# Two-layer GLA and differential-attention network with hierarchical experts: gather banks, order of the opening, and the residual's place

## Chip, cores and metric

One core of a Trainium2 chip runs the whole program. The metric is the device time of one execution in microseconds. TensorE (PE) does the matmuls, VectorE (DVE) and ScalarE (ACT) the elementwise work and the copies out of the matmul accumulators (PSUM), SyncE (SP) issues the DMAs that load the weights, and GpSimd (POOL) does little.

## What is computed

The input is 256 tokens of width 1024, in fp32. Layer 0 mixes tokens by gated linear attention, layer 1 by differential attention on keys and values made from layer 0's output. Behind each mixer stands a layer norm of the scaled residual, then a mixture of 16 experts (two per token, from one of four groups of four), and another residual and norm:

```
for layer in range(DEPTH):                       # DEPTH = 2
    mix = gla_mixer(h, ...) if layer < 1 else diff_attention(h, ..., k1, k2, v, ...)
    h = layer_norm(ALPHA * h + mix, ln_g[layer, 0], ln_b[layer, 0])       # ALPHA = sqrt 2
    ffn = hier_moe(h, ...)
    h = layer_norm(ALPHA * h + ffn, ln_g[layer, 1], ln_b[layer, 1])

def hier_moe(t):                                 # 256 x 1024
    combine = ...                                # 256 x 16, two weights per token
    y = 0
    for e in range(16):
        hdn = silu(t @ w_gate[e]) * (t @ w_up[e])        # 1024 x 512 each
        y = y + combine[:, e:e + 1] * (hdn @ w_down[e])  # 512 x 1024
```

## The kernel before

The mixers take the first 131 us and the stretch from about 365 to 504 us; the change does not touch them. The rest is the function moe, once per layer.

**One expert.** Each expert has a block of 64 slots. A one-hot matrix OH says which token sits in which slot. Of an expert, PE does, in this order: the transposes of the expert before's scatter matrix and hidden values (s_prep L594 and tr_part L626, into PSUM banks of tag pC), the first quarter of its gate and up products (gu_part L610, j = 0, into a bank of tag pB), the down product of the expert before (down_part L638, one pB and one pC bank), the other three quarters of gate and up, and the scatter of the expert before (L670: four matmuls that add the product o into the four accumulators y of tag pA, which stay open through all experts). DVE and ACT make silu and the product (L617, L619), copy transposes out (L629), and split the down product into a rounded high and a low part o (ACT L646, DVE L647), since fp32r matmuls keep only the high part. PE runs its instructions in program order. The loop at L766 issues all this; "with after(x)" puts an instruction behind x in the order. An fp32 matmul leaves two records in the profile, an fp32r one (gather, scatter, broadcasts) one. Expert matmuls use half of the array's columns, c = 0 and c = 1, and two of them, one on each half, run side by side.

**The gather.** For every four experts gather_group (L538) makes their inputs xg: 32 matmuls of the split x (tile xs: high part by ACT L534, low part by DVE L535, four buffers) with OH, in eight steps k of four (high and low part of each token half), two steps to a bank. Of each bank DVE copies one half out (L562), then ACT the other (L560). It stands at the opening of moe and behind the transposes in the iterations e = 4, 8 and 12; in layer 1 the last gather also makes the inputs of a seventeenth block (five blocks, one step to a bank). All these banks are of tag pC, of which there are two; pB has two as well, used in turn by gate and up products and down products. At the opening, DVE makes the first token half of OH (L519), the low parts of the first four xs, then the second half of OH.

**The residual.** ALPHA times the normed input must be added to y. At e = 5 the generator residual (L408) rebuilds it in the tile xr: eight broadcast matmuls of the norm's weights (bcast_row L203, two per bank, four banks of pC), each bank read by two DVE instructions (L417 or L419), then the subtraction of the mean (L424). Then, for each of its four blocks of 512 columns, ACT L809 writes a high part and DVE L810 a low part into two tiles of tag o (two buffers, shared with the down products), and two identity matmuls L812 add them to y.

**Weights.** SP loads an expert as six tiles of 1 MB (four for gate and up in two DMAs each, two for down), into a ring of 16 slots; three spare tiles x0 to x2 take weights 16 to 18 of each layer and are free afterwards. A slot's next load starts when PE has read its last one. So weights come in as PE uses them up.

## Time and profile before

| | us |
|---|---|
| median of 3 runs | 770.43 (769.76 to 772.49) |
| the profiled execution | 771.24 |
| its span, first to last instruction | 769.3 |
| PE busy | 727.1 (95%) |
| DVE busy | 357.4 (46%) |
| ACT busy | 296.8 (39%) |
| experts of layer 0, opening gather to last scatter | 132 to 366 |
| experts of layer 1 | 504 to 758 |

PE is busy nearly everywhere, so idle time alone says little: a busy PE includes pairs that run one by one. The better measure is the distance from one expert's scatter to the next, which is the same for all ordinary experts, and what stands between where it is longer. In the rows further down, x16 counts records, a time in brackets is the idle time before a group and what ended it, PEclk is the clock granted to TensorE as a share of full speed, and the DMA share is the mean busy share of the core's 16 DMA engines.

### The profile page before, as it was taken

To read this page: it belongs to the slowest core of one execution; us is meant where nothing else is said; L and a number is where in the kernel's file an instruction comes from. 1 tells how busy PE (TensorE), PEld (TensorE's weight loads), DVE (VectorE), ACT (ScalarE), POOL (GpSimd) and SP (SyncE) were. 2 spreads that over 40 slices of the span, in tenths; PEclk is the share of its full clock that TensorE was granted. 3 is DMA by queue.
4 is the path that set the end of the run, shared out by engine and by line. 5 is a ranking of instruction groups with operands and counts; after the bars stand their busy time and mean duration, and the time that the engine had idled before them with its cause. 6 is when DMAs were issued, how large, how long until landed. Compare 5 with 4: busy or idle time off the path is not lost. (4 is left out here: it accounts for less than half of the span.)

```text
span 769.3 us, 10560 instructions
## 1 busy us (share of the span) xinstructions
PE 727.1 (95%) x3743; PEld 407.8 (53%) x3743; DVE 357.4 (46%) x959; ACT 296.8 (39%) x651; POOL 8.9 (1%) x21
## 2 busy tenths in 40 slices
PE   7999998999999999999999999999999999999993
PEld 5898776434333434434798877753343343343331
DVE  3655766333263332322758877654235332332225
ACT  4554766323212322222666656552232232232123
POOL 2200000000000000000000000000000000000000
PEclk9999999999999999999999999999999999999997
DMA  7999957599999999999999355619999999999951
GB/s 226 312 384 388 337 191 262 181 397 394 367 387 392 393 396 395 393 393 367 290 364 359 111 174 209 220 62 389 394 381 395 393 363 384 395 395 393 392 200 55
DMA packets 131934, 247.57 MB, mean 322 GB/s; under 512 B 7932, under 2 KB 38117, under 8 KB 131750
## 3 DMA queue, kind: packets, MB, share of 16 engines
q1 hardware_dynamic: 131270, 244.68, 87.6%
q0 software_dynamic: 176, 1.59, 0.5%
q8 instruction: 31, 0.51, 0.3%
q10 hardware_dynamic: 432, 0.59, 0.2%
q14 instruction: 25, 0.20, 0.1%
HBM read 245.77 MB, written 2.63 MB: 323 GB/s over the span
## 5 line engine op out<-in xcount | busy, mean ns | idle before, releaser
L610 PE MATMUL pB<-W,xg 128*64 128x512 f32 x1056 | 263.6, 600 | 0.0
L610 PEld LDWEIGHTS pB<-W,xg 128*64 128x64 f32 x1056 | 77.3, 138 | 137.9 <-issue 132.3
L638 PE MATMUL pB<-W,ht 128*64 128x512 f32 x248 | 112.6, 594 | 0.0
L638 PE MATMUL pC<-W,ht 128*64 128x512 f32 x248 | 111.5, 592 | 0.0
L647 DVE SCALAR_TENSOR_TENSOR o<-pB,wst,o 64x512 fp32r<-64x512 f32 x31 | 23.1, 744 | 145.3 <-ACT o L646 145.3
L119 DVE TENSOR_TENSOR lo<-W,hi 128x512 fp32r<-128x512 f32 x96 | 66.4, 696 | 37.0 <-PE pA L128 23.9
L118 ACT ACTIVATE hi<-W 128x512 fp32r<-128x512 f32 x96 | 59.3, 629 | 48.3 <-PE pA L129 27.8
L646 ACT ACTIVATE o<-pB,wst 64x512 fp32r<-64x512 f32 x31 | 21.2, 682 | 129.6 <-PE pC L638 101.8
L619 DVE TENSOR_TENSOR hd<-sl,pB 128x256 f32<-128x256 f32 x33 | 13.9, 421 | 102.5 <-ACT sl L617 102.5
L617 ACT ACTIVATE sl<-pB 128x256 f32<-128x256 f32 x33 | 12.7, 385 | 126.0 <-PE pB L610 126.0
L638 PEld LDWEIGHTS pB<-W,ht 128*64 128x64 f32 x248 | 33.3, 137 | 52.4 <-issue 49.3
L553 PE MATMUL pC<-OH,xs 128*128 128x256 f32 (+1 forms) x256 | 39.7, 308 | 7.4 <-DVE ht L629 3.8
L670 PE MATMUL pA<-o,st 128*128 128x512 f32 x132 | 40.9, 431 | 4.3 <-DVE o L664 2.1
L553 PEld LDWEIGHTS pC<-OH,xs 128*128 128x128 f32 x256 | 34.8, 203 | 17.8 <-DVE ht L629 5.2
L638 PEld LDWEIGHTS pC<-W,ht 128*64 128x64 f32 x248 | 33.9, 137 | 19.4 <-issue 18.2
L670 PEld LDWEIGHTS pA<-o,st 128*128 128x128 f32 x132 | 22.4, 191 | 33.3 <-issue 23.5
L129 PE MATMUL pA<-x1Thi,lo 128*128 128x256 f32 x128 | 36.1, 288 | 1.4 <-DVE lo L119 1.2
L127 PE MATMUL pA<-x1Thi,hi 128*128 128x256 f32 x128 | 36.7, 288 | 0.0
L128 PE MATMUL pA<-x1Tlo,hi 128*128 128x256 f32 x128 | 36.2, 284 | 0.0
L128 PE MATMUL pA<-lo,xThi 128*128 128x384 f32 (+1 forms) x96 | 34.3, 357 | 0.0
L129 PE MATMUL pA<-hi,xTlo 128*128 128x384 f32 (+1 forms) x96 | 34.3, 357 | 0.0
L127 PE MATMUL pA<-hi,xThi 128*128 128x384 f32 (+1 forms) x96 | 34.2, 362 | 0.0
(338 smaller groups left out, 1086.2 us busy)
## 6 DMA issues: line engine op xcount, KB each, us to landing
W<-in_moe_w_gate_dram SPq DMA_DIRECT2D x132, 512.0 KB, 11.2
W<-in_moe_w_up_dram SPq DMA_DIRECT2D x132, 512.0 KB, 11.0
W<-in_moe_w_down_dram SPq DMA_DIRECT2D x66, 1024.0 KB, 12.0
W<-in_a_w_in_dram SPq DMA_DIRECT2D x16, 256.0 KB, 5.6
W<-in_a_w_in_dram SPq DMA_DIRECT2D x4, 1024.0 KB, 17.8
W<-in_a_w_out_dram SPq DMA_DIRECT2D x4, 1024.0 KB, 14.4
W<-in_kv_w_dram SPq DMA_DIRECT2D x4, 1024.0 KB, 8.8
W<-in_b_w_q_dram SPq DMA_DIRECT2D x16, 256.0 KB, 5.4
```

What stands on the lines that cost most here:

```text
L118: act.activation(hi, src, AF.Copy)
L119: dve.tensor_sub(lo, src, hi)
L127: pe.matmul(o, l[0], r[0], start=first, stop=False, skip_group_check=skip)
L128: pe.matmul(o, l[0], r[1], start=False, stop=False, skip_group_check=skip)
L129: pe.matmul(o, l[1], r[0], start=False, stop=last, skip_group_check=skip)
L553: pe.matmul(o, xs[k][:, q // 2, q % 2], OH[g][:, q % 2].rearrange("p e s -> p (e s)"), start=q == 0, stop=q == 3)
L610: mm = pe.matmul(p[c * m:c * m + m, 0:2 * fw].rearrange("p (g f) -> p g f", g=2), xg(k), w[:, :, kk, c * fw:c * fw + fw], start=k == 0, st ...
L619: anchor[1] = dve.tensor_mul(h, sl, p[:, fw:2 * fw])
L638: mm = pe.matmul(p[2 * c // nt][c * m:c * m + m, 0:w], ht[:, q % n, (q // n) * m:(q // n) * m + m], wd_[q // 2][:, q % 2, c * w:c * w + w] ...
L646: act.activation(hi, src, AF.Copy, scale=ws[a:a + m, 0:1])
L647: dve.scalar_tensor_tensor(lo, src, ws[a:a + m, 0:1], hi, op0=ALU.mult, op1=ALU.subtract)
L670: mm = pe.matmul(y[b][c], st[:, b * 128:b * 128 + 128], o[c], start=False, stop=last, skip_group_check=True)
```

## The change

Four edits, all in moe and residual:

1. gather_group takes its banks in the order pB, pB, pC, pC (and again from the start for the gather of five).
2. At the opening, the low parts of xs 1 to 3 are issued behind the second half of OH.
3. The matmuls of down_part are chained in their order, so that its pB and pC products always alternate.
4. The residual is spread. Its first four steps (columns 0 to 511) stand behind the transposes of e = 5, the rest behind those of e = 6; their broadcasts use pB and pC in turn. The high and low parts of one token block (512 KB of fp32r) go to a spare tile rs, block 0 at e = 6 and block 1 at e = 7, and are added by four identity matmuls each (L805) behind the scatters in the iterations e = 7 and e = 8. The tag o is no longer used for it.

```diff
--- before.py
+++ after.py
@@ -405,13 +405,13 @@
         dve.tensor_scalar(gsub, pb[:, P_GS:P_GS + 1], 1.0 - LAM0, None, op0=ALU.mult)
         return nlam, gsub
 
-    def residual(idx, dst):
+    def residual(idx, dst, tiles=(pC, pC)):
 
         s = sm([128, 2, 2], "hsum2")
         for h in range(2):
             hs = slice(h * 512, h * 512 + 512)
             for i in range(2):
-                p = bcast_row(8 * i + 2 * idx + h, pC)
+                p = bcast_row(8 * i + 2 * idx + h, tiles[i])
                 for b in range(2):
                     if i == 0:
                         dve.scalar_tensor_tensor(dst[:, b, hs], xa[:, b, hs], ALPHA, p, op0=ALU.mult, op1=ALU.mult)
@@ -526,13 +526,16 @@
 
             lows = []
 
-            def split_x(k, eng, hold=None):
+            def split_x(k, eng, hold=None, later=False):
 
                 t = mp.tile([128, 2, 2, 128], F32R, tag="xs", bufs=4, name=nm("xs"))
                 x_ = xa[:, :, k * 128:k * 128 + 128]
                 with after(hold):
                     act.activation(t[:, 0], x_, AF.Copy)
-                lows.append(eng.tensor_sub(t[:, 1], x_, t[:, 0]))
+                low = lambda: lows.append(eng.tensor_sub(t[:, 1], x_, t[:, 0]))
+                if later:
+                    return t, low
+                low()
                 return t
 
             def gather_group(g, hold=None, xs=()):
@@ -545,7 +548,9 @@
                 xs = list(xs)
                 for k in range(KC):
                     if n == 5 or k % 2 == 0:
-                        p = pC()
+
+                        i = k if n == 5 else k // 2
+                        p = pC() if i // 2 % 2 else pB()
                     if k >= len(xs):
                         xs.append(split_x(k, dve, hold))
                     o = p[:, 0:320] if n == 5 else p[:, k % 2 * 256:k % 2 * 256 + 256]
@@ -633,10 +638,12 @@
 
                 m, n, w = 128 // nt, 4 // nt, D // nt
                 p = [pB(), pC()]
+                mm = None
                 for q in range(4):
                     for c in range(nt):
-                        mm = pe.matmul(p[2 * c // nt][c * m:c * m + m, 0:w], ht[:, q % n, (q // n) * m:(q // n) * m + m], wd_[q // 2][:, q % 2, c * w:c * w + w],
-                                  start=q == 0, stop=q == 3)
+                        with after(mm):
+                            mm = pe.matmul(p[2 * c // nt][c * m:c * m + m, 0:w], ht[:, q % n, (q // n) * m:(q // n) * m + m], wd_[q // 2][:, q % 2, c * w:c * w + w],
+                                            start=q == 0, stop=q == 3)
                 warm(filler, mm)
                 o = [mp.tile([128, 512], F32R, tag="o", bufs=2, name=nm("o"))[0:2 * m] for _ in range(2)]
                 for c in range(nt):
@@ -756,9 +763,16 @@
                 ht, _ = tr_part(act_part(p, 2), 2)
                 scatter(st, down_part(wdn, ht, wsx, 2)[0], True)
 
-            xs0 = [split_x(k, dve) for k in range(4)]
+            xs0, rest = [split_x(0, dve)], []
+            for k in range(1, 4):
+                t, low = split_x(k, dve, later=True)
+                xs0.append(t)
+                rest.append(low)
             act.activation(sm([128, 2], "warm"), xs0[3][:, 0, 0, 0:2], AF.Exp, scale=0.0)
-            one_hot(0)
+
+            with after(one_hot(0)):
+                for low in rest:
+                    low()
             gather_group(0, None, xs0)
             with after(lows[3]):
                 cw = combine()
@@ -784,6 +798,11 @@
                 with after(mm):
                     if prev is not None:
                         mm = scatter(prev[1], o, False)
+                    if e in (7, 8):
+
+                        with after(mm):
+                            for i in range(4):
+                                mm = pe.matmul(y[e - 7][i // 2], ident_r, rs[:, i // 2, i % 2], start=False, stop=False, skip_group_check=True)
                     with after(mm):
                         sp_ = s_prep(lambda b: OH[g][:, b, e - 4 * g], 64, cw[:, :, e] if e < E else extra[2], anchor)
                     with after(sp_[2]):
@@ -798,18 +817,25 @@
                 if e in (1, 5, 9):
                     held[e + 3] = anchor[0], anchor[1]
                 if e == 5:
+
                     xr = spare_tile(2, [128, 2, D], F32, "xr")
-                    for _ in residual(2 * layer, xr):
-                        pass
-
-                    for b in range(2):
-                        for h in range(2):
-                            v = xr[:, b, h * 512:h * 512 + 512]
-                            hi, lo = (mp.tile([128, 512], F32R, tag="o", bufs=2, name=nm("res")) for _ in range(2))
-                            act.activation(hi, v, AF.Copy)
-                            dve.tensor_sub(lo, v, hi)
-                            for a in (hi, lo):
-                                pe.matmul(y[b][h], ident_r, a, start=False, stop=False, skip_group_check=True)
+                    steps = residual(2 * layer, xr, (pB, pC))
+                    with after(mm):
+                        for _ in range(4):
+                            next(steps)
+                if e == 6:
+                    with after(mm):
+                        for _ in steps:
+                            pass
+                if e in (6, 7):
+                    b = e - 6
+                    rs = spare_tile(1, [128, 2, 2, 512], F32R, "rs")
+                    for h in range(2):
+                        v = xr[:, b, h * 512:h * 512 + 512]
+                        with after(anchor[0] if e == 7 else None):
+                            act.activation(rs[:, h, 0], v, AF.Copy)
+                        with after(anchor[1] if e == 7 else None):
+                            dve.tensor_sub(rs[:, h, 1], v, rs[:, h, 0])
                 if e == 9 and layer:
                     gb = spare_tile(0, [128, 2, 2, 512], F32, "gb")
                     for i in range(2):
```

The order of DVE at the opening of layer 0, before (posm gives the slot of each token, xs_1696 to 1705 are the four split tiles):

```order
L510 SCALAR_TENSOR_TENSOR posm_1694<-sel_1685,pC_1688 128x32
L519 TENSOR_TENSOR OH_1710<-posm_1694,cb 128x256
L535 TENSOR_TENSOR xs_1696<-xa,xs_1696 128x256
L535 TENSOR_TENSOR xs_1699<-xa,xs_1699 128x256
L535 TENSOR_TENSOR xs_1702<-xa,xs_1702 128x256
L535 TENSOR_TENSOR xs_1705<-xa,xs_1705 128x256
L519 TENSOR_TENSOR OH_1710<-posm_1694,cb 128x256
```

and after:

```order
L510 SCALAR_TENSOR_TENSOR posm_1694<-sel_1685,pC_1688 128x32
L519 TENSOR_TENSOR OH_1707<-posm_1694,cb 128x256
L535 TENSOR_TENSOR xs_1696<-xa,xs_1696 128x256
L519 TENSOR_TENSOR OH_1707<-posm_1694,cb 128x256
L535 TENSOR_TENSOR xs_1699<-xa,xs_1699 128x256
L535 TENSOR_TENSOR xs_1701<-xa,xs_1701 128x256
L535 TENSOR_TENSOR xs_1703<-xa,xs_1703 128x256
```

The second OH row has moved from behind four xs rows to behind one.

The order of PE at the second gather (e = 4, layer 0), before:

```order
L594 MATMUL pC_1999<-ident_r,ohw_1996 128x128 x2
L626 MATMUL pC_2006<-ident_r,hd_1990 128x128 x2
L553 MATMUL pC_2015<-OH_2011,xs_2016 128x256 x4
L553 MATMUL pC_2015<-OH_2011,xs_2023 128x256 x4
L553 MATMUL pC_2032<-OH_2011,xs_2033 128x256 x4
L553 MATMUL pC_2032<-OH_2011,xs_2040 128x256 x4
L610 MATMUL pB_2083<-W_992,xg_2014 64x512
L553 MATMUL pC_2049<-OH_2011,xs_2050 128x256 x4
L553 MATMUL pC_2049<-OH_2011,xs_2057 128x256 x4
L553 MATMUL pC_2066<-OH_2011,xs_2067 128x256 x4
L553 MATMUL pC_2066<-OH_2011,xs_2074 128x256 x4
L610 MATMUL pB_2083<-W_992,xg_2014 64x512 x3
```

and after:

```order
L631 MATMUL pC_2006<-ident_r,hd_1990 128x128 x2
L558 MATMUL pB_2015<-OH_2011,xs_2016 128x256 x4
L558 MATMUL pB_2015<-OH_2011,xs_2023 128x256 x4
L558 MATMUL pB_2032<-OH_2011,xs_2033 128x256 x4
L558 MATMUL pB_2032<-OH_2011,xs_2040 128x256 x4
L558 MATMUL pC_2049<-OH_2011,xs_2050 128x256 x4
L558 MATMUL pC_2049<-OH_2011,xs_2057 128x256 x4
L558 MATMUL pC_2066<-OH_2011,xs_2067 128x256 x2
L615 MATMUL pB_2083<-W_992,xg_2014 64x512
L558 MATMUL pC_2066<-OH_2011,xs_2067 128x256 x2
L558 MATMUL pC_2066<-OH_2011,xs_2074 128x256 x4
L615 MATMUL pB_2083<-W_992,xg_2014 64x512 x3
```

The first sixteen gather matmuls now write pB banks, and the lone gate and up matmul of the next expert (W is its weights) stands ten gather matmuls further on.

The order of PE at the residual, in the iteration e = 6 of layer 0, before (o and res share a tag; y is pA_1654 to 1657):

```order
L610 MATMUL pB_2246<-W_1024,xg_2014 64x512 x3
L203 MATMUL pC_2197<-lnr,sel_r 128x256 x2
L203 MATMUL pC_2202<-lnr,sel_r 128x256 x2
L610 MATMUL pB_2246<-W_1024,xg_2014 64x512
L638 MATMUL pB_2251<-W_1020,ht_2193 64x512 x2
L203 MATMUL pC_2207<-lnr,sel_r 128x256 x2
L638 MATMUL pB_2251<-W_1022,ht_2193 64x512
L203 MATMUL pC_2212<-lnr,sel_r 128x256 x2
L638 MATMUL pB_2251<-W_1022,ht_2193 64x512
L638 MATMUL pC_2252<-W_1020,ht_2193 64x512 x2
L638 MATMUL pC_2252<-W_1022,ht_2193 64x512 x2
```

and after:

```order
L203 MATMUL pB_2197<-lnr,sel_r 128x256 x2
L615 MATMUL pB_2207<-W_1024,xg_2014 64x512
L203 MATMUL pC_2202<-lnr,sel_r 128x256 x2
L615 MATMUL pB_2207<-W_1024,xg_2014 64x512 x3
L645 MATMUL pB_2212<-W_1020,ht_2193 64x512
L645 MATMUL pC_2213<-W_1020,ht_2193 64x512
L645 MATMUL pB_2212<-W_1020,ht_2193 64x512
L645 MATMUL pC_2213<-W_1020,ht_2193 64x512
L645 MATMUL pB_2212<-W_1022,ht_2193 64x512
L645 MATMUL pC_2213<-W_1022,ht_2193 64x512
L645 MATMUL pB_2212<-W_1022,ht_2193 64x512
```

Four broadcasts (lnr is the norm's weights) have moved to the next expert; down products alternate between pB and pC. The identity matmuls, which before stood one by one within the gate and up products, now stand behind a scatter, here that of e = 7:

```order
L677 MATMUL pA_1654<-o_2298,st_2254 128x512
L677 MATMUL pA_1655<-o_2299,st_2254 128x512
L677 MATMUL pA_1656<-o_2298,st_2254 128x512
L677 MATMUL pA_1657<-o_2299,st_2254 128x512
L805 MATMUL pA_1654<-rs,ident_r 128x512 x2
L805 MATMUL pA_1655<-rs,ident_r 128x512 x2
L599 MATMUL pC_2331<-ident_r,ohw_2328 128x128 x2
L631 MATMUL pC_2338<-ident_r,hd_2318 128x128 x2
```

The eight matmuls of x2 and x2 rows are split over two experts; the other four stand one expert later. SP's and POOL's orders are unchanged.

## Rows read from the trace of the kernel before

**Rows 1.** The page, busy time, share of the span and instructions of an engine.

```profile
PE 727.1 (95%) x3743; PEld 407.8 (53%) x3743; DVE 357.4 (46%) x959; ACT 296.8 (39%) x651; POOL 8.9 (1%) x21
```

**Rows 2.** Timeline of PE, opening of layer 0 (start us, us, ..., [idle <-releaser]).

```profile
132.64 0.51 PE L553 MATMUL pC<-OH,xs 128*128 128x256 f32 x2
134.27 3.36 PE L553 MATMUL pC<-OH,xs 128*128 128x256 f32 x14 [1.12 <-DVE OH L519]
...
138.65 2.18 PE L553 MATMUL pC<-OH,xs 128*128 128x256 f32 x16
140.75 0.65 PE L610 MATMUL pB<-W,xg 128*64 128x512 f32 x2
```

**Rows 3.** Timeline of DVE, same stretch.

```profile
132.46 1.42 DVE L535 TENSOR_TENSOR xs<-xa,xs 128x256 fp32r<-128x256 f32 x4
133.80 0.41 DVE L519 TENSOR_TENSOR OH<-posm,cb 128x256 fp32r<-128x256 f32 x1
```

**Rows 4.** Windows of 6 us: busy us per engine, PEclk, DMA share, GB/s.

```profile
132.00:138.00 6.00, 4.85 (x20) 3.79 (x19) 4.18 (x15) 3.52 (x8) 0.00 (x0) 0.72 0.01 3
...
330.00:336.00 6.00, 6.00 (x32) 2.50 (x30) 2.21 (x6) 0.95 (x3) 0.00 (x0) 1.00 1.04 396
...
606.00:612.00 6.00, 4.14 (x13) 2.55 (x14) 3.16 (x6) 2.03 (x5) 0.00 (x0) 0.72 1.02 401
```

**Rows 5.** Timeline of PE, layer 0, second gather.

```profile
185.28 1.21 PE L670 MATMUL pA<-o,st 128*128 128x512 f32 x4
...
187.55 2.18 PE L553 MATMUL pC<-OH,xs 128*128 128x256 f32 x16 [0.63 <-DVE ht L629]
189.71 1.07 PE L610 MATMUL pB<-W,xg 128*64 128x512 f32 x2
190.72 2.17 PE L553 MATMUL pC<-OH,xs 128*128 128x256 f32 x16
...
203.26 0.98 PE L670 MATMUL pA<-o,st 128*128 128x512 f32 x3
```

**Rows 6.** Timeline of PE, layer 1, the gather of five blocks.

```profile
684.91 1.64 PE L553 MATMUL pC<-OH,xs 128*128 128x320 f32 x8 [0.45 <-ACT xg L560]
```

**Rows 7.** Timeline of PE, the residual's experts in layer 0, then layer 1.

```profile
215.29 1.21 PE L670 MATMUL pA<-o,st 128*128 128x512 f32 x4
...
218.73 0.72 PE L203 MATMUL pC<-lnr,sel_r 64*128 64x256 f32 x4
...
237.44 1.51 PE L670 MATMUL pA<-o,st 128*128 128x512 f32 x4 [1.06 <-DVE o L647]
...
267.76 1.21 PE L670 MATMUL pA<-o,st 128*128 128x512 f32 x4
...
586.74 1.21 PE L670 MATMUL pA<-o,st 128*128 128x512 f32 x4
...
640.26 1.19 PE L670 MATMUL pA<-o,st 128*128 128x512 f32 x4
```

**Rows 8.** The residual's splits by line: count, ns min/median/max, starts, form.

```profile
L809 ACT ACTIVATE res<-xr x8: 621/629/632, 225.5 to 606.0; 128x512 fp32r<-128x512 f32 x8
...
L810 DVE TENSOR_TENSOR res<-xr,res x8: 684/691/695, 226.4 to 606.6; 128x512 fp32r<-128x512 f32 x8
```

**Rows 9.** SP's queue: issues of late weight loads, layer 0, then layer 1.

```profile
340.42 0.60 SPq L282 DMA_DIRECT2D W<-in_moe_w_up_dram  x1
...
729.15 0.74 SPq L733 DMA_DIRECT2D W<-in_moe_w_down_dram  x1
```

**Rows 10.** DMA issues of these two: KB, us from issue to landing.

```profile
W<-in_moe_w_up_dram SPq DMA_DIRECT2D x1, 512.0 KB, 10.8
...
W<-in_moe_w_down_dram SPq DMA_DIRECT2D x1, 1024.0 KB, 13.0
```

**Rows 11.** Timeline of PE where these two are used.

```profile
352.27 5.32 PE L610 MATMUL pB<-W,xg 128*64 128x512 f32 x24
...
751.67 0.43 PE L658 MATMUL pB<-W,ht 128*64 128x256 f32 x1 [0.63 <-DVE ht L629]
```

## The prediction

> **What bounds the kernel now.** I read the page first: PE is busy 95% of the span [rows 1], so a gain must come out of PE's stream. Then PE's timeline, from one scatter to the next. An ordinary expert takes 12.03 us: 215.29 less 203.26 [rows 5, 7]. An expert with a gather takes 17.98 (185.28 to 203.26) [rows 5], and the three experts from the one with the residual to the third gather of layer 0 take 52.47 (215.29 to 267.76), where three ordinary ones would take 36.09 [rows 7]. In layer 1 the same three take 53.52 (586.74 to 640.26) [rows 7]. These excesses, 5.95, 16.38 and 17.43 us, are what the change can work on, and the opening. Last, the weights: in the middle of the experts the DMA engines have a share of 1.04 and move 396 GB/s [rows 4]. An expert's six tiles are 6.3 MB (six of 1024 KB), so at that rate 15.9 us; PE uses them up in 12.03. So the lead of the weights shrinks from expert to expert, and what is left of it at the end of a layer limits what PE can gain.
>
> **The opening, twice.** PE does two gather matmuls, then waits 1.12 us for the second half of OH, then does fourteen in 3.36 us, and sixteen more in 2.18 [rows 2]. Sixteen in 2.18 are 0.136 each; fourteen should take 1.9. The mean granted clock of these 6 us is 0.72, against 1.00 later [rows 4]: behind the wait PE ran at the lower of its two levels. DVE does four low parts in 1.42 us ahead of that half of OH, which starts at 133.80 [rows 3]. With one ahead of it, it starts at 132.46 + 0.36 = 132.82 and ends by 133.23, so the wait falls to about 0.15. The three low parts behind it end by 134.3; PE needs the last of them about twelve matmuls later. The gather then takes 0.5 (the first two, with the rest of the wait) + 4.4 (32 by 0.136) + 1.0 (the lone gate and up matmul in the middle, 1.01 from 189.71 to 190.72 [rows 5]) = 5.9 from 132.64, to 138.6; before, PE goes on at 140.75 [rows 2]. That is 2.15 us in each layer. Bounds: 1.0 if only OH comes earlier and the clock falls all the same, 2.2 at best.
>
> **The gathers.** The second one waits 0.63 us for the copy of the transposes, because it needs the pC bank that they stand in [rows 5]. Now its first two banks are pB: one held the gate and up product of the expert just finished, which DVE read before the transposes could start, the other a down product of the expert before, long copied. The third bank is pC, but comes 2.17 us later [rows 5]. So 0.6 goes; nothing is late in its place, since the xs and OH are made experts ahead. I take 0.57. The lone matmul stays lone, and stands ten gather matmuls later, so it has more time for the two copies ahead of it. The last gather of layer 0 saves the same. That of layer 1 has eight banks, and besides the 0.63 waits at least once more for ACT, 0.45 [rows 6]: with four banks in turn both should go, 1.0. What it adds: pB now takes turns between gathers and products, and the first product of the expert reuses the first gather bank. That is costed among the rivals.
>
> **The residual and the third gather.** Before: 16.38 us of excess in layer 0, of which 5.95 is the gather. The rest is four broadcast matmuls of 0.18 (0.72 for four [rows 7]) and two more pairs inside the down product, whose halves then run alone instead of in pairs; eight identity matmuls one by one among the gate and up products; and at the end the scatter waits 1.06 for the down product's low part [rows 7], since the splits of the residual stand ahead of it and share its two tiles. Layer 1 loses 1.05 more, and there the clock is 0.72 over 606 to 612 [rows 4]. After:
> - Experts 5 and 6 each get four broadcasts, 0.72, and between them one gate and up matmul alone, 1.01 against 0.44 in the stream (24 records in 5.32, two to a matmul [rows 11]): 1.3 each, 2.6.
> - Four identity matmuls behind a scatter, twice. Four scatter matmuls of the same form take 1.21 [rows 7]: 2.4.
> - The third gather, 5.95 less 0.57 = 5.4. Just ahead of it ACT and DVE have the second block's splits, 2 by 0.629 and 2 by 0.691 [rows 8], and these can't start before PE has read the first block, since rs is one tile. Bounds: 0, or all four in a row, 2.6. PE has half a gather, 2.17, to do meanwhile, in banks that are free, so I take 0.5.
>
> Together 10.9. DVE's other new work (four reads and two subtractions) lies in the 12 us of an expert in which it has at most half to do [rows 1]. So layer 0 saves 16.38 - 10.9 = 5.5 and layer 1 17.43 - 10.9 = 6.5. The chain in down_part keeps the pairing that ordinary experts have already: nothing, or 0.4 either way for an expert. SP issues the same loads in the same order, each when its slot comes free.
>
> **What the weights allow.** PE's sum is 2.15 + 0.57 + 5.5 + 0.57 = 8.8 in layer 0 and 2.15 + 0.57 + 6.5 + 1.0 = 10.2 in layer 1. In layer 0 the last up tile is issued at 340.42 [rows 9] and lands 10.8 later [rows 10], at 351.2. PE starts the last quarter of its products two thirds into the 5.32 us from 352.27 [rows 11], at 355.8: a lead of 4.6 us. The stream of loads starts when PE has used up its first tile, so 2.15 earlier with the shorter opening, and after that it is full. So PE can come 4.6 + 2.15 = 6.75 us earlier and no more: layer 0 saves 6.75, and PE waits about 2 us for weights at its end. In layer 1 the last down tile lands at 729.15 + 13.0 = 742.2 [rows 9, 10], for use from 751.67 on [rows 11], a lead of 9.5; with 2.15 it is 11.6, more than 10.2. So layer 1 keeps all of it.
>
> By the Trainium skill (HBM Reference, Specifications) a core that streams alone measures about 425 GB/s. At that rate, an estimate from that page, an expert would take 14.8 us instead of 15.9, the lead would shrink more slowly, and layer 0 would save its whole 8.8. The rows have 396, and I go by them.
>
> **The sum.** 6.75 + 10.2 = 17 us. The profiled execution took 771.24, so 754.3; it was 0.8 above the median of 770.43, which gives 753.5. I forecast 753.5.
>
> **Rivals.**
> 1. *The weights give way.* The stream had short holes in which slots were not yet free, and a faster PE closes them, or the late loads land sooner. Then layer 0 saves 8.8, and with 0.5 more at each third gather the whole is 20: 750.5. For it: the lead is bounded from medians of single loads. Against it: 1.04 at 330 to 336 [rows 4].
> 2. *Part of the gain stays away.* The clock falls at the opening all the same (1.15 less in each layer; it then also holds back the stream of layer 0), and the third gather queues behind the splits for the full 2.6 (2.1 more in layer 1; in layer 0 the weights hide about half). Sum: 6.75 - 1.15 and 10.2 - 1.15 - 2.1, together 12.5: 758. For it: at the opening DVE still has low parts, copies and the weights' softmax to do in a row.
> 3. *The weights bound both layers.* Then only the earlier start of the stream counts, 2.15 twice: 766. For it: a DMA share of 1.02 to 1.04 in the middle [rows 4]. Against it: the leads of 4.6 and 9.5 us, which a bound kernel would not have. The Trainium skill (Perfetto Trace Analysis, Identifying the Most-Contended Engine) has DMA judged by the share of HBM bandwidth and has the most contended engine improved first; by it this stage is the DMA's, and a gain on PE is worth nothing.
> 4. *Slower.* The first gate and up product needs the gather's first bank, and the down product the second. If PE stands until DVE's and ACT's copies of each are out, and the copies queue behind splits and low parts, each gather adds two such waits. The nearest row is the opening's 1.12 [rows 2], and behind such a wait the clock fell, 3.36 for 1.9: 1.46 more. Twice 1.12 and 1.46 are 3.7; at eight gathers 29.6, less the 17: about 783. It decides from 2.1 us per gather. Against it: between the bank's last matmul and its next use stand eighteen gather matmuls, 2.4 us, and one copy by each engine takes less than half of that.
> 5. *It does not do what it says*: PE takes up the same waits elsewhere (low parts instead of OH, rs instead of o), and nothing moves: 770.
>
> **How the numbers follow.** The forecast (751.5 to 756.5) has 0.46, rival 1 0.21, rival 2 0.19, rival 3 0.06, rival 4 0.04, rival 5 0.04. About 0.5%, 3.9 us, is what a measurement of this kernel can tell from no change, so faster is below 766.6: the first three and half of the third rival, 0.89. Same: the other half and rival 5, 0.07. Slower 0.04. The range reaches from rival 1 with the best openings, 748.5, to rival 2 with the gather of five unchanged as well and the residual's experts costing 2 us more, 761.
>
> **What would show it.** In the opening, the wait for OH falls from 1.12 to below 0.3, the granted clock over the 6 us is near 1.00, and the stream of gate and up goes on about 5.9 us after the first gather matmul. Scatters: about 13.3 us apart around experts 5 and 6 (12.03 + 1.3), about 17.4 at a plain gather, 18 to 20 at the third. No stretch at 0.72 around the residual of layer 1. In the last experts of layer 0 PE waits for a weight DMA, about 2 us in all; without such waits rival 1 is right, with more than 4 rival 3. A wait for ACT's copy ahead of the first gate and up product of a group's first expert speaks for rival 4. The forecast is wrong if the leads of the weights were not what holds layer 0, or if PE's waits only change their names.

## The result, and the profile after

The changed kernel takes 752.73 us (median of 4 runs, 750.7 to 753.64) against 770.46 before: a ratio of 0.9764, 95% interval 0.975 to 0.9777. Its profiled execution took 753.32, with a span of 751.7; that is 17.6 less span than before. The forecast was 753.5.

The page has the same PE share as [rows 1], in a shorter span; in the windows (busy us of PE, PEld, DVE, ACT and POOL, PEclk, DMA share, GB/s) the clock is now full at the opening and at 606, where [rows 4] had 0.72, and low at two other places. 0.72 is a mean over six us: TensorE has two levels, 1.2 and 2.4 GHz, and in a window that lies wholly in such a stretch (342 to 344) the granted clock is 0.50, the lower one; below this is called half clock.

```profile
PE 717.3 (95%) x3743; PEld 407.7 (54%) x3743; DVE 355.6 (47%) x959; ACT 293.2 (39%) x651; POOL 8.9 (1%) x21
```

```profile
132.00:138.00 6.00, 5.66 (x34) 4.04 (x34) 5.19 (x16) 4.52 (x11) 0.00 (x0) 1.00 0.01 3
...
339.00:345.00 6.00, 4.99 (x16) 1.97 (x18) 0.00 (x0) 0.00 (x0) 0.00 (x0) 0.72 1.05 387
360.00:366.00 6.00, 5.38 (x17) 4.08 (x16) 5.00 (x14) 3.02 (x7) 0.31 (x2) 0.72 1.12 290
606.00:612.00 6.00, 6.00 (x37) 4.32 (x32) 2.79 (x7) 2.98 (x9) 0.00 (x0) 1.00 1.05 387
```

PE's timeline at the opening (start, us, idle before and its releaser), to be set against [rows 2]: the wait for OH is gone, sixteen matmuls run in one piece, and the products go on at 138.67.

```profile
132.84 2.57 PE L558 MATMUL pB<-OH,xs 128*128 128x256 f32 x16
135.24 0.40 PE L558 MATMUL pC<-OH,xs 128*128 128x256 f32 x2
135.80 1.07 PE L615 MATMUL pB<-W,xg 128*64 128x512 f32 x2 [0.16 <-ACT xg L565]
136.80 1.94 PE L558 MATMUL pC<-OH,xs 128*128 128x256 f32 x14
138.67 2.79 PE L615 MATMUL pB<-W,xg 128*64 128x512 f32 x12
```

The same engine at the second gather, at the first half of the residual, and at the third gather with the first residual block, to be set against [rows 5, 7]. No wait stands ahead of L558 any more; the scatter at 239.97 waits for nothing; the four matmuls L805 take 0.93 (241.01 to 241.94, where the transposes follow).

```profile
183.18 1.19 PE L677 MATMUL pA<-o,st 128*128 128x512 f32 x4
...
184.56 2.16 PE L558 MATMUL pB<-OH,xs 128*128 128x256 f32 x16
186.56 1.39 PE L558 MATMUL pC<-OH,xs 128*128 128x256 f32 x10
187.88 1.07 PE L615 MATMUL pB<-W,xg 128*64 128x512 f32 x2
...
212.25 1.19 PE L677 MATMUL pA<-o,st 128*128 128x512 f32 x4
...
213.81 0.50 PE L203 MATMUL pB<-lnr,sel_r 64*128 64x256 f32 x2
214.23 1.07 PE L615 MATMUL pB<-W,xg 128*64 128x512 f32 x2
215.23 0.50 PE L203 MATMUL pC<-lnr,sel_r 64*128 64x256 f32 x2
...
239.97 1.20 PE L677 MATMUL pA<-o,st 128*128 128x512 f32 x4
241.01 1.09 PE L805 MATMUL pA<-rs,ident_r 128*128 128x512 f32 x4
241.94 0.38 PE L599 MATMUL pC<-ident_r,ohw 128*128 128x128 f32 x2
...
245.43 1.07 PE L615 MATMUL pB<-W,xg 128*64 128x512 f32 x2 [0.27 <-ACT xg L565]
```

And the end of layer 0. Before, the same products (from 347.07 on) waited for nothing:

```profile
347.07 1.94 PE L610 MATMUL pB<-W,xg 128*64 128x512 f32 x8
348.83 0.59 PE L638 MATMUL pB<-W,ht 128*64 128x512 f32 x1
...
366.32 5.26 PE L181 MATMUL pB<-zero_r 128*128 128x512 f32 x23 [0.53 <-ACT warm L830]
```

After, PE stands for 2.44 us until the last expert's first up tile has landed. Behind it the clock is low (a down product takes 1.06 instead of 0.59), and again at 361, where 23 matmuls by zero take 6.93 instead of 5.26.

```profile
337.19 0.38 PE L631 MATMUL pC<-ident_r,hd 128*128 128x128 f32 x2
340.01 2.76 PE L615 MATMUL pB<-W,xg 128*64 128x512 f32 x8 [2.44 <-DMA W<-in_moe_w_up_dram]
342.50 1.06 PE L645 MATMUL pB<-W,ht 128*64 128x512 f32 x1
...
361.03 6.93 PE L181 MATMUL pB<-zero_r 128*128 128x512 f32 x23 [0.62 <-ACT warm L856]
```

Stage by stage, from the starts of the scatters (first scatter of a layer less first gather matmul, and so on), the two profiled executions differ by:

| stage | before, us | after, us | change | forecast |
|---|---|---|---|---|
| start to first gather matmul | 132.64 | 132.84 | +0.2 | 0 |
| opening of layer 0, to its first scatter | 27.29 | 25.00 | -2.29 | -2.15 |
| its second gather | 17.98 | 17.05 | -0.93 | -0.57 |
| residual and third gather, four scatter distances | 64.50 | 59.20 | -5.30 | -5.5 |
| last gather | 17.60 | 16.40 | -1.20 | -0.57 |
| last expert's weights (12.03 to 16.24) | 12.03 | 16.24 | +4.21 | +2.05 |
| between the layers | 139.60 | 141.00 | +1.40 | 0 |
| opening of layer 1 | 27.24 | 24.94 | -2.30 | -2.15 |
| its experts, first to last scatter | 225.04 | 213.70 | -11.34 | -8.05 |

### The profile page after: what moved, and what is told of

It is laid out like the page before. It is cut to its first block, busy times and chain, and to the rows that moved or that the text cites. A ratio compares the mean times of both kernels' runs of the same rounds, so it can differ in the third digit from the quotient of the medians.

```text
span 751.7 us, 10554 instructions
## 1 busy us (share of the span) xinstructions
PE 717.3 (95%) x3743; PEld 407.7 (54%) x3743; DVE 355.6 (47%) x959; ACT 293.2 (39%) x651; POOL 8.9 (1%) x21
## 5 line engine op out<-in xcount | busy, mean ns | idle before, releaser
L605 ACT ACTIVATE pC<-pC 128x256 f32<-128x256 f32 x33 | 12.1, 368 | 38.0 <-DVE st L602 37.3
L129 PEld LDWEIGHTS pA<-x1Thi,lo 128*128 128x128 f32 x128 | 24.1, 191 | 3.2 <-DVE lo L119 2.6
```

What stands on the lines that cost most here:

```text
L129: pe.matmul(o, l[1], r[0], start=False, stop=last, skip_group_check=skip)
```

## The experiments

**One part alone.** Three kernels with one part of the change each, and one with two of them.

Banks alone:

```diff
-                        p = pC()
+                        i = k if n == 5 else k // 2
+                        p = pC() if i // 2 % 2 else pB()
```

> Only the gathers' banks (pB, pB, pC, pC) are changed. Theory (PE's stream sets the time, and in layer 0 the weights' lead of some 5 us caps the gain): the three later gathers of a layer lose their wait for the transposes' copy, about 0.9 us each, and the last ones 1.2 and 2.4 as in the changed kernel: 3.1 us in layer 0, 4.3 in layer 1, together 7.4, so 763. No wait for weights in layer 0, since 3.1 is less than the lead. Rival (the weights hold both layers): nothing moves, 770. Rival (the products that share pB wait for the gathers' copies): slower than 770.

Measured: 762.5 us, ratio 0.9905 (0.9886 to 0.9924). Second and third gathers cost 17.05 and 17.08 from scatter to scatter, the last one 16.41, and 18.10 in layer 1: as expected, with no wait for weights. So the shared pB holds nobody up. That the time itself is near the expected 763 says less: in the profiled execution (760.72) both openings are 1.4 shorter as well (25.91 for 27.29 in layer 0), with the wait for OH as before (1.16) but a full clock, and stretches at half clock stand elsewhere (at 234 and 602).

Opening alone:

```diff
-            xs0 = [split_x(k, dve) for k in range(4)]
+            xs0, rest = [split_x(0, dve)], []
...
-            one_hot(0)
+            with after(one_hot(0)):
+                for low in rest:
+                    low()
```

> Only the order of DVE at the opening is changed (second half of OH ahead of three low parts). Theory: the wait of 1.12 us for OH goes and the granted clock stays at 1.00 there; 2.1 us in each layer, 4.2 to 4.6 in all, so 766. Rival (the clock falls at that place whatever PE waits for): 1.0 in each layer, 768.5, and a mean clock near 0.72 in the 6 us from the first gather matmul on.

Measured: 770.38 us, ratio 1.0001 (0.999 to 1.0013). Both theories miss. PE's timeline shows why the edit alone has nothing to give: the wait for OH is gone here too, but with two pC banks alone the order of PE falls out otherwise. Beside the lone gate and up matmul between the halves of the gather (136.61), which stood there before too, two more (139.00 and 140.67) stand alone within the second half, about 1 us each.

```profile
134.12 2.56 PE L556 MATMUL pC<-OH,xs 128*128 128x256 f32 x16
136.61 1.07 PE L613 MATMUL pB<-W,xg 128*64 128x512 f32 x2
137.61 1.45 PE L556 MATMUL pC<-OH,xs 128*128 128x256 f32 x10
139.00 1.07 PE L613 MATMUL pB<-W,xg 128*64 128x512 f32 x2
140.00 0.74 PE L556 MATMUL pC<-OH,xs 128*128 128x256 f32 x4
140.67 1.07 PE L613 MATMUL pB<-W,xg 128*64 128x512 f32 x2
```

In this profiled execution the openings are still 1.0 shorter than in that of before (26.30 for 27.29 in layer 0), since the clock is full there; other stretches at half clock (at 32 and 236) take it back.

Residual alone, with the chain (the hunks on residual, on down_part and on the loop):

```diff
+                    if e in (7, 8):
+                        with after(mm):
+                            for i in range(4):
+                                mm = pe.matmul(y[e - 7][i // 2], ident_r, rs[:, i // 2, i % 2], start=False, stop=False, skip_group_check=True)
...
+                    rs = spare_tile(1, [128, 2, 2, 512], F32R, "rs")
```

> Only the residual is moved (with the chained down products), gathers keep pC alone and the opening its order. Theory: the three experts from the residual on to the third gather lose 4.4 us in layer 0 and 5.4 in layer 1 (0.9 less than in the changed kernel, the gather's own part), about 10 in all: 760.5, a little more if a stretch at the lower clock goes with it. The weights' lead in layer 0 just about covers 4.4. Together with the other two parts alone the sum is then about 22 us against 17.7 measured for all: the rest is what the weights take back in layer 0. Rival (no cap by weights): the three parts alone add up to 17.7 within the interval.

Measured: 758.33 us, ratio 0.9847 (0.9822 to 0.9873), the largest part. The four scatter distances around the residual fall from 64.50 to 59.54 in layer 0 and from 65.53 to 59.56 in layer 1, 5.0 and 6.0 for the 4.4 and 5.4 expected. At the end of layer 0 PE already waits for weights, if less than in the changed kernel:

```profile
342.01 1.94 PE L610 MATMUL pB<-W,xg 128*64 128x512 f32 x8 [1.06 <-DMA W<-in_moe_w_up_dram]
```

The opening's order and banks are as they were. There PE waits for OH as before, 1.15 us; but the fourteen matmuls behind take 1.93 and not 3.36, and the window has a clock of 1.00:

```profile
132.78 0.48 PE L553 MATMUL pC<-OH,xs 128*128 128x256 f32 x2
134.41 1.93 PE L553 MATMUL pC<-OH,xs 128*128 128x256 f32 x14 [1.15 <-DVE OH L519]
```

```profile
132.00:138.00 6.00, 4.71 (x25) 3.10 (x26) 5.49 (x19) 4.66 (x11) 0.00 (x0) 1.00 0.01 3
```

Neither expected sum came out. By medians the three parts gain 7.9, 0.0 and 12.1, together 20.1, and banks with opening (below) and residual 22.4, against 17.7 for all. The weights take back only 1.4 of this (2.44 of wait for 1.06). The third gather takes back 1.2 in the two layers: behind the moved residual the banks save 0.3 there (18.85 to 18.52), not 0.9. For what is left the medians show no cause; in the profiled executions it is stretches at half clock: before has four outside the start and the end, residual alone one, banks with opening two, so that some of them count in both gains.

Banks and opening together (the first two diffs):

> The gathers' banks and the order of DVE at the opening, without the residual's move. From the profiles of the two parts alone, first gather matmul to first scatter takes 25.90 us with the banks alone, 26.30 with the order alone, 25.00 in the changed kernel. Theory (the order pays only with the banks, 0.9 in each layer): 1.8 below the banks alone at 762.5, so 760.7, and 25.0 in this stretch. Rival (the parts add up as measured alone, the order being worth nothing): 762.5.

Measured: 760.11 us, ratio 0.986 (0.9842 to 0.9878). The stretch from first gather matmul to first scatter took 25.00 us in layer 0. With the clock full, that stretch is 25.96 with neither edit (residual alone), 25.91 with the banks, 26.30 with the order, 25.00 with both: the order pays 0.9 only where the banks are there. The measured time and this stretch agree with the theory.

**The chain of the down products, undone.**

```diff
-                mm = None
...
-                        with after(mm):
-                            mm = pe.matmul(p[2 * c // nt][c * m:c * m + m, 0:w], ...
+                        mm = pe.matmul(p[2 * c // nt][c * m:c * m + m, 0:w], ...
```

> The changed kernel without the chain of the down products. Its order differs at one expert of each layer (the down product next to the first half of the residual), whose four pB and four pC products then run alone and not in pairs. Theory: eight products of 0.43 us in place of four pairs cost about 1.7 us of PE in each layer; layer 1 pays it, layer 0 does not, since there PE waits for weights by more than that near its end: 1.7 above the changed kernel, 754.5. Rival (layer 0 isn't held by weights): 3.4 above, 756. Rival (the chain is worth nothing, as the prediction had it): 752.7.

Measured: 753.79 us, ratio to before 0.9792 (0.9773 to 0.9812), 1.06 above the changed kernel's median, whose own runs spread over 2.9. In the profile the expert at the residual's first half costs 15.65 us instead of 13.86 in both layers, 1.8 more, since the down products run in rows of one bank, which here is one half of the array's columns:

```profile
217.50 2.31 PE L643 MATMUL pC<-W,ht 128*64 128x512 f32 x5
...
220.56 1.88 PE L643 MATMUL pB<-W,ht 128*64 128x512 f32 x4
```

In layer 0 this is given back: the distance ahead of the last expert is 12.73 instead of 16.24. The wait for weights is 0.63 there instead of 2.44, and the clock stays full. So layer 0 hides 1.8 us of extra PE work, as it must if weights end it. The medians alone would not tell 754.5 from the rivals: stretches at half clock lie elsewhere in this execution too (one of 1.6 at e = 9 of layer 1, none at layer 0's end).

**Fewer weights in layer 0.**

```diff
                 if e == 8 and j == 0:
                     yield
+                if layer == 0 and e == 10 and j in (2, 3):
+                    gu.append(gu[1])
+                    continue
                 n += 1
```

> The changed kernel with two weight tiles fewer in layer 0: the third and fourth quarter of expert 10's gate and up products read the second quarter's tile again, so 2 of its 100 MB are not loaded and this part of the output is another. PE's work is unchanged. Theory (late weights are what layer 0 lost at its end): every later load lands some 5 us sooner, the wait of 2.44 us ahead of the last expert's first product goes, and with it the stretch at the lower clock behind it; the distance of the last two scatters before the last expert falls from 16.24 to 12.03, and the time by 4 us or a little more, to about 748. Rival (the wait is a single transfer's bad luck or something else on PE): no change, 752.7.

Measured: 748.06 us, ratio 0.9721 (0.9701 to 0.9742), 4.7 below the changed kernel. The last expert's first product follows the transposes at once, and the distance of scatters is 12.03:

```profile
337.62 0.38 PE L634 MATMUL pC<-ident_r,hd 128*128 128x128 f32 x2
337.93 1.94 PE L618 MATMUL pB<-W,xg 128*64 128x512 f32 x8
```

This decides for the weights: nothing of PE's work was changed. A single transfer's bad luck is out as well: five kernels here wait at this place, and in each PE goes on 13.35 to 13.37 us after the issue of the same tile (326.66 and 340.01 in the changed kernel).

**The stream started sooner.**

```diff
+                    if k == 4 and mid:
+                        last = mid(t)
...
+            def begin(t):
+                first.append(pB())
+                first.append(gu_part(M[0][0], (0,), lambda k: t[:, k, 0:64], first[0], 2))
+                return first[1]
+            gather_group(0, None, xs0, begin)
```

> The changed kernel with the first quarter of the first expert's gate and up products put between the two halves of the opening's gather, as two pairs, where before one matmul of it stood alone there and three behind. PE does the same matmuls, 0.57 us sooner for the pair. But the first weight tile is used up about 2.3 us sooner (135.8 + 0.9 for 139.1), so the stream of loads starts so much sooner in each layer. Theory (in layer 0 the start and the rate of the stream set when the last expert can begin): its wait falls from 2.44 to near 0.1, the stretch at the lower clock behind it goes too: 4 us from there, and 0.5 from layer 1's opening: 748. Rival (only PE's own time counts): 0.57 in each layer, 751.6.

Measured: 751.46 us, ratio 0.9753 (0.9726 to 0.9781): the rival's number. The wait at the end of layer 0 is the same 2.42. The head start is lost on the way: at 192 to 198 the stream has a hole, for want of free slots, and moves 307 GB/s, where the changed kernel moves 379. The first row and the wait are this kernel's, the last row is the changed kernel's.

```profile
192.00:198.00 6.00, 6.00 (x32) 2.00 (x30) 1.50 (x2) 1.37 (x2) 0.00 (x0) 1.00 0.92 307
```

```profile
339.90 1.94 PE L619 MATMUL pB<-W,xg 128*64 128x512 f32 x8 [2.42 <-DMA W<-in_moe_w_up_dram]
```

```profile
192.00:198.00 6.00, 6.00 (x31) 1.99 (x29) 1.50 (x2) 1.37 (x2) 0.00 (x0) 1.00 1.03 379
```

The eight records behind this wait take 1.94, not 2.76: the clock stayed full.

SP's queue shows how the head start is lost. In each kernel it stands at the second gather until PE has read out a slot. The first load behind that and, far later, the last expert's first up tile go out at these times before, in the changed kernel and here:

```profile
194.78 0.37 SPq L282 DMA_DIRECT2D W<-in_moe_w_gate_dram  x1
329.87 0.43 SPq L282 DMA_DIRECT2D W<-in_moe_w_up_dram  x1
```

```profile
191.75 0.37 SPq L282 DMA_DIRECT2D W<-in_moe_w_gate_dram  x1
326.66 0.40 SPq L282 DMA_DIRECT2D W<-in_moe_w_up_dram  x1
```

```profile
191.64 0.37 SPq L282 DMA_DIRECT2D W<-in_moe_w_gate_dram  x1
326.53 0.43 SPq L282 DMA_DIRECT2D W<-in_moe_w_up_dram  x1
```

PE comes to the second gather only 0.13 sooner here than in the changed kernel (183.05 for 183.18), and that is all that the late loads gain.

**The wait filled.**

```diff
-                        ht, mm = tr_part(h, 2)
+                        ht, mm = tr_part(h, 2, 10 if layer == 0 and e == 14 else 0)
```

> The changed kernel with ten matmuls by zero (2.2 us) into the accumulators, behind the transposes of layer 0's expert 14, where PE otherwise waits for weights. They change no result. Theory (the stretch at the lower clock behind the wait comes from the wait): the clock stays at 1.00 there, 1.7 us less behind it, and perhaps the one at 360 to 365 too: 751 or 749.5. Rival (the clock falls by its own schedule, as at the opening, where it fell in one kernel and not in another behind the same wait): no change, 752.7; or 2 us more if the matmuls hold up the products.

Measured: 751.75 us, ratio 0.9761 (0.9743 to 0.9778). The clock was full at both places, and PE still waited 1.15 us for the tile behind the ten matmuls. But the clock was full in the kernel with the earlier stream as well, where PE idled for 2.42. So this run can't tell whether the filling did it: inconclusive, and within the runs' spread.

**Longer pieces of weights.** Two neighbouring rows to a partition, with the columns of x, of the norm's weights and of the hidden values taken in the same order.

```diff
-                        sp.dma_start(t[:, gi], w[layer, e, j * 256:j * 256 + 256].rearrange("(k p) f -> p k f", p=128))
+                        sp.dma_start(t[:, gi], w[layer, e, j * 256:j * 256 + 256].rearrange("(p k) f -> p k f", p=128))
...
-                x_ = xa[:, :, k * 128:k * 128 + 128]
+                x_ = xa[:, :, k // 2 * 256:k // 2 * 256 + 256].rearrange("p b (c i) -> p b c i", i=2)[:, :, :, k % 2]
```

> The changed kernel with expert weights laid out otherwise in the tiles: each partition takes two neighbouring rows of the matrix (4 KB of gate or up, 8 KB of down in one piece of memory) in place of two rows 128 apart (2 and 4 KB); the columns of x and of the hidden values are taken in the same order, so nothing is left out. Theory (the stream's rate bounds layer 0): if longer pieces move faster than the 396 GB/s seen, by 3% or more, an expert's weights take 0.5 us less, the wait at the end of layer 0 goes, and the time is about 748; PE pays for reading every second column in the splits at most 1 us. Rival (the rate is set elsewhere): 396 GB/s again and 752.7 to 753.5.

Measured: 750.12 us, ratio 0.9742 (0.9716 to 0.9769). The stream moves 406 GB/s from 150 to 330 us, at a lower busy share, against 392 in the changed kernel; first this kernel, then that one:

```profile
150.00:330.00 180.00, 179.64 (x852) 76.02 (x850) 65.33 (x158) 46.70 (x105) 0.52 (x1) 1.00 1.01 406
```

```profile
150.00:330.00 180.00, 179.65 (x854) 75.36 (x852) 65.31 (x158) 46.24 (x105) 0.52 (x1) 1.00 1.04 392
```

These rows take in the hole at the second gather, which is deeper here (251 GB/s at 192 to 198). Behind it the difference is larger, 4.8%:

```profile
210.00:330.00 120.00, 119.64 (x568) 51.20 (x566) 46.62 (x111) 31.32 (x72) 0.52 (x1) 1.00 1.02 411
```

```profile
210.00:330.00 120.00, 119.64 (x570) 50.82 (x568) 45.62 (x109) 30.87 (x71) 0.52 (x1) 1.00 1.04 392
```

There is no wait for weights at the end of layer 0 (12.04 to the last but one scatter), and PE pays 0.07 at an opening for the other reading order. The time is 2 us above the 748 expected; the profiled execution has a stretch at half clock at 33 to 37 us, before anything that differs.

**A version that beats both.** Longer pieces, the early first quarter, the first products of a group's first expert behind the whole gather, and layer 1's last broadcasts in pB and pC:

```diff
-                    with after(prev and prev[4]):
+                    with after(gm if e in (4, 8, 12) else prev[4]):
...
-                            act.activation(gb[:, i, h], bcast_row(8 * i + 4 * layer + 2 + h, pC), AF.Copy)
+                            act.activation(gb[:, i, h], bcast_row(8 * i + 4 * layer + 2 + h, (pB, pC)[h]), AF.Copy)
```

> The kernel with 4 KB and 8 KB pieces of weights (750.1) with three more edits: the first quarter of the first expert's products between the halves of the opening's gather (0.57 us of PE in each layer); the first gate and up products of a group's first expert behind the whole gather, in pairs, in place of one alone in its middle (0.57 at each of three gathers in a layer, less where PE then waits for the last low parts); and the broadcasts of layer 1's output norm in pB and pC (0.6 to 1.1). Theory (with the faster stream layer 0 has 5.5 us of lead left at its last expert, so PE's time counts again in both layers): 1.1 + 2.5 to 3.4 + 0.8, some 5 us, 745. Rival (the weights take it back in layer 0): 747.

Measured: 744.5 us, ratio to before 0.9663 (0.9637 to 0.9688), 8.2 below the changed kernel. The second gather costs 16.40, the third 17.7 with a residual block; layer 1's last broadcasts cost 0.8 less (14.08 for 14.86). The last gathers gained next to nothing (16.40 as in the changed kernel, 18.04 for 18.11), so the 745 came with a part of its sum missing. At layer 0's last expert nothing waits:

```profile
335.36 0.41 PE L637 MATMUL pC<-ident_r,hd 128*128 128x128 f32 x2
335.69 1.94 PE L621 MATMUL pB<-W,xg 128*64 128x512 f32 x8
```

## Why the prediction was right

**The sum held, by terms that erred both ways.** Forecast 17 us off the profiled execution, measured 17.9 (771.24 less 753.32). That the two agree so well is in part luck, as the terms show.

- *Opening.* Sized right, 2.15 against 2.3, but its cause was half wrong. The step "behind the wait PE ran at the lower of its two levels" made the clock a part of the edit's worth. Residual alone has neither of the two edits here and the same wait, but a full clock: with that alone the stretch is 1.3 us shorter (25.96 for 27.29), and the two edits together pay 0.96. The rest of the 2.3 is a stretch at half clock that fell there in the profiled execution of before. That the order of DVE alone earns this was wrong: at a full clock it lengthens the stretch by 0.3 without the banks.
- *Gathers.* 0.57 was 0.93: besides the wait of 0.63 the ordinary step from transposes to the next bank shrank (184.43 to 184.56, where an expert without a gather has 0.3). The last gathers saved 1.2 and 2.4 (20.55 to 18.11) for 0.57 and 1.0; I had priced only the one wait for ACT in [rows 6], and in layer 0's gather the second half's waits not at all.
- *Residual.* 10.9 us of cost forecast, 11.1 measured in layer 0 (59.20 less four times 12.03), made up otherwise. The experts with broadcasts cost 1.83 more each for 1.3; an addition costs 0.93 for 1.2; and the third gather costs 5.57 for 5.9 (18.53 less 12.03 and 0.93). That is 0.55 more than the second gather costs in the same kernel, near the 0.5 taken for the splits; 0.27 of it is seen as a wait.
- *Chain.* "Nothing, or 0.4 either way" was wrong. It is worth 1.8 us at one expert in each layer, and a glance at the order without it would have shown the rows of one bank.
- *Weights.* That layer 0 would end on weights and layer 1 would not was right, and fewer weights show it as a cause. PE comes to the last expert's first product 7.06 us sooner (347.07 to 340.01), where 6.75 was allowed. But the nearness is luck, since two steps of the working were off and nearly cancel. I took the lead at the last expert's last up tile, 4.6. It was the first tile that held PE; if it landed 13.35 after its issue at 329.87 before too, as where PE waits for it, its lead was 3.85 (an estimate). And I let the stream start 2.15 sooner and stay full. In truth the load behind the hole at the second gather went out 3.03 sooner (194.78 to 191.75), 2.10 because PE came to that gather sooner and 0.93 because the gather is shorter; the late loads are 3.21 sooner. 3.85 and 3.21 make the 7.06. An earlier start that doesn't bring PE sooner to that gather is worth nothing to the late loads (the experiment on it).
- *What the wait cost.* Forecast 2.05 at layer 0's end, measured 2.44 of wait and 1.77 of half clock behind it, and 1.40 at 360. Layer 1's broadcasts at e = 9, on the other side, lost 1.63 in before at half clock (16.49 for 14.86) and did not in after, with the same waits. Outside the start and the end there are four such stretches in the execution of before (1.3 in each opening, 1.1 at 608, 1.63 at 656) and two in that of after (1.77 and 1.40). So some 2.2 of the 17.9 come from the clock, which no run ties to the edits; the forecast had counted 3.3 on it (1.15 in each opening and 1.05 at layer 1's residual), and these errors nearly cancel.

What stays open is why the clock falls at one place in one kernel and not in another. Behind a wait of 1.12 to 1.16 at the opening it fell in before and not with the residual or the banks alone; behind 2.44 and 2.42 at layer 0's end it fell in after and not with the early stream. So a wait of that length doesn't settle it, and no run here did. It also differs between executions of one kernel: those of before, measured beside the parts, go from 768.13 us at a mean granted clock of 0.990 to 771.45 at 0.985.

Of the rivals, the weights holding both layers (3) is out: layer 1 took its whole gain, 13.6 us, under the same DMA share (1.05 at 606 to 612). The weights giving way (1) is out too, since PE waited 2.44 for them. pB as a new wait (4) is out by the banks alone, and that nothing moves (5) by the result. Of rival 2, that a part stays away, the clock came true, if elsewhere, and the queue behind the splits for 0.55 us where it had 2.6.

## What to carry to other kernels

Where loads run in a ring that PE empties, work out PE's gain and the lead of the loads apart, and take the smaller; then test with fewer loads, since PE's own timeline shows the wait only after it has come. A lead made at the start is lost at the next place where the ring is full, while a better rate is kept. Two edits at one place can be worth nothing or less alone and 0.96 us together, so look at the order that each gives, and don't count a stretch at half clock as a part of what an edit earns before a second kernel has shown it there.

## What the runs showed of the hardware

- Pieces of 4 and 8 KB in place of 2 and 4 KB raised the stream from 392 to 411 GB/s (4.8%, 210 to 330 us) at a DMA share of 1.02 instead of 1.04. A share above 1.00 did not mean that no more could be moved.
- A stretch at half clock (granted 0.50) costs 1.1 to 1.8 us here and comes up to four times in an execution of these kernels outside its ends (four in before, two in after, one with the residual alone, none with fewer weights), at different places in kernels whose code there is the same.
